# Gate stage: the residual rows are added by accumulating transfers, and each tile is finished one pair later

## The chip, the cores and the metric

The kernel runs on one core of one Trainium2 chip. The metric is the device time of one execution in microseconds. A core has a matrix engine (PE, with its weight loads shown as PEld), a vector engine (DVE), a scalar engine (ACT), a general engine (POOL) and a sync engine (SP) that only issues transfers. Each executes its own instructions in order; semaphores tie them together. Transfers are issued from the queues of SP, POOL and ACT and are carried out by 16 DMA engines that all queues share.

## The reference

One layer of a streaming encoder over 2048 prompt rows and 32 sample rows of width 1024:

```
hn = rmsnorm(h);  proj = hn @ w_in
yA, yB = short-conv mixer(proj), pooling mixer(proj)
h = h + concat[yA, yB] @ w_out
gate = sigmoid(rmsnorm(h) @ w_ple_gate)
h = h + (p @ w_ple) * gate
y = rmsnorm(h) * g_final
```

All of it is in 32-bit floating point, and the small state outputs of the two mixers are returned too. The change touches only the last two lines: `h + e*gate` with `e = p @ w_ple`, and the final norm.

## The kernel before

The rows are cut into 16 tiles of 128 rows (0 to 15) and one of 32 rows (16). Products are made at full precision from pairs of rounded numbers: each operand is split into a high and a low part, and three matmuls stand for one. Pairs of tiles are multiplied with seven block products instead of eight, after Strassen and Winograd, in the function `seven`.

The program has three stages. The first makes the input projection and the mixers, about 0 to 520 us. The second multiplies by w_out and adds the input, giving h, which is stored in device memory as `h_d`; interleaved with it, e is made and stored as `e_d`. The third, the gate stage, starts at 729.6 us and works through the tiles in pairs: the pairs 0, 2, 4 to 12 in the loop at L1809, and the pair 14 with tile 15 in `last_pair`, which ends the program. The 32-row tile is done by itself between pairs 4 and 6 (`short_gate`).

For a pair i the gate stage does this. Two "frames" (`hn` tiles) are loaded from `h_d` ahead of time in `prep_g`: the upper tile i by one transfer (L396), the lower one i + 1 by four that rearrange it (L1512). The upper frame is copied by ACT (L1552) and transposed on PE (L1554, `pth`); the lower one is transposed on DVE (L1560). Sums and differences of the blocks are formed (L1743) and split into high and low parts (L81 on ACT, L84 on DVE). Then `seven` issues the products, 12 matmuls each, in the order 11, 12, S2, S1, S3, S4, 22; the places between them are numbered, and `following[st]` runs what is wanted at place st. Results in PSUM (X, Y, Z) are copied out by ACT (`c_g`, L1573) or added by DVE (L1581), and go through the sigmoid on ACT (L1582 or L1579). In `gate_ops`, DVE multiplies the half tile of e by the gate (L1584) and adds the product to the half tile of h (L1585), four times each for a pair. `done_g` then finishes a tile: ACT squares and sums it (L94), POOL makes the reciprocal root (L73 and L77), DVE multiplies by both factors (L1592), and the tile is stored to the output (L1593).

Tiles of 128 x 1024 live in rings: `xh` with four tiles holds the two h tiles of a pair, and `ya` with five holds frames and e tiles. A tile's place is free again when its last reader is done, which for a stored tile is when the store has landed. The order of instructions on each engine comes from a scheduler that works ahead of time with its own estimates of durations; `tc.keep_in_program_order` pins an instruction to its place in the program. Order is thus fixed at build time, and a wait at run time holds everything behind it on the same engine.

h tiles of pairs 0 to 4 are loaded from POOL's queue, the others from SP's. Output tiles 0 to 5 and 16 are stored from POOL's queue, 6 to 15 from SP's, the very last piece from ACT's.

Of the kernel before, what the change touches and what calls it, by code (L numbers as in the profile page):

```python
# [15 lines left out]
P = 128  # L16
# [20 lines left out]
def trunk(ctx, tc, x_p, x_s, c_conv, c_pool, p_p, p_s, g_mix, w_in, conv_w, conv_b, pool_w,  # L37
# [1266 lines left out]
    with ExitStack() as s2:  # L1304
# [202 lines left out]
        def by_quarters(i):  # L1507

            r, n = tiles[i]
            t = ring4(ya, f"hn_{i}")  # L1510
            for q in range(4):
                nc.sync.dma_start(t[q * 32:q * 32 + 32].rearrange("p (g c) -> p g c", g=4),  # L1512
                                  h_d[r:r + P, q * 256:q * 256 + 256].rearrange("(g p) c -> p g c", p=32))
            return t
# [53 lines left out]
        def gate_ops(h, e, n, name, i):  # L1568
            scale = lambda at: rs_h[:n, i + at[0]:i + at[0] + 1]

            def carry(ps, at):
                t = st.tile([P, NH], F32, tag="t", name=f"c_{name}_{at[0]}{at[1]}")
                carried.append(nc.scalar.copy(t[:n], ps[:n]))  # L1573
                return t

            def out(ps, c, at):
                if c is None:
                    c = st.tile([P, NH], F32, tag="t", name=f"g_{name}_{at[0]}{at[1]}")
                    nc.scalar.activation(c[:n], ps[:n], AF.Sigmoid, scale=scale(at))  # L1579
                else:  # L1580
                    nc.vector.tensor_tensor(c[:n], ps[:n], c[:n], op=ALU.add)  # L1581
                    nc.scalar.activation(c[:n], c[:n], AF.Sigmoid, scale=scale(at))  # L1582
                ee, hh = half_of(e, at, n), half_of(h, at, n)
                nc.vector.tensor_tensor(ee, ee, c[:n], op=ALU.mult)  # L1584
                nc.vector.tensor_tensor(hh, hh, ee, op=ALU.add)  # L1585

            return carry, out

        def done_g(i, h, later=False):
            r, n = tiles[i]  # L1590
            rf = sumsq(h, n, f"f{i}", later=later)
            nc.vector.scalar_tensor_tensor(h[:n], h[:n], rf[:n], g_bc[:n], op0=ALU.mult, op1=ALU.mult)  # L1592
            (nc.sync if 6 <= i < NT - 1 else nc.gpsimd).dma_start(rows_of(y_p, y_s, r, n), h[:n])  # L1593

        def short_ops(h, e, n):

# [13 lines left out]

            return carry, out

        def last_pair(i, A, before):

# [112 lines left out]
                weigh(1, cols_of(0))  # L1727
                normed(1, root(1))

            seven(f"g{i}", A, W, held, out, {1: chunk, 3: before, 4: rest, 5: upper_half}, first_tile=True, end=end)  # L1730

        def prep_g(i, ahead=False):

            A, got = {}, {}
            whole = lambda t: t.rearrange("p k (g t) -> p k g t", g=4)

            def put(q, src, view=lambda t: t):
                A[q] = cmb.tile([P, KH, 2, P], F32R, tag="c", name=f"g{i}_{q}")
                split(view(A[q][:, :, 0]), view(A[q][:, :, 1]), src)

            def comb(q, x, y, op, view=lambda t: t):
                t = ss.tile([P, KH, P], F32, tag="s", name=f"g{i}_f{q}")
                nc.vector.tensor_tensor(view(t), x, y, op=op)  # L1743
                return t

            lower = []

            def load():
                got["lower"] = by_quarters(i + 1) if i else first_lower
                got["upper"] = load_rows(ya, "hn", i, h_d) if i else first_h  # L1750

            if ahead:
                load()

            def first():
                if not ahead:
                    load()
                lower.extend(turned_here(got["lower"], not i))

            def second():  # L1760
                a21, a22 = lower
                s1 = comb("S1", a21, a22, ALU.add, whole)
# [12 lines left out]
            S[i] = A  # L1775
            return {2: first, 4 if i in (2, 8) else 3: second}
# [20 lines left out]
        def short_gate():  # L1797
# [7 lines left out]
            done_g(NT - 1, h)  # L1805
            yield

        short_steps = short_gate()
        for i in range(0, NT - 3, 2):  # L1809
            A = S.pop(i)  # L1810
            following = prep_g(i + 2, not i)
            h = [load_rows(xh, "h", i + b, h_d, queue=nc.gpsimd if i < 6 else nc.sync) for b in range(2)]
            e = [load_rows(ya, "e", i + b, e_d) for b in range(2)]
            seven(f"g{i}", A, W, *gate_ops(h, e, P, f"g{i}", i), following)
            done_g(i, h[0])
            if i in (0, 2, 4):
                next(short_steps)
            if i + 2 < NT - 3:
                done_g(i + 1, h[1])
        last_pair(NT - 3, S[NT - 3], lambda: done_g(NT - 4, h[1], True))  # L1820

# [1 line left out]
_INS = ['x_prompt', 'x_sample', 'cache_conv', 'cache_pool', 'p_prompt', 'p_sample', 'g_mix', 'w_in',  # L1823
# [25 lines left out]
```

## Time and profile before

| what | value |
|---|---|
| median of 3 runs | 909.32 us (908.84 to 909.93) |
| profiled execution, its own time | 909.97 us |
| profiled execution, span of instructions | 908.2 us |
| PE busy | 893.2 us, 98% of the span |
| DVE busy | 702.4 us, 77% |
| ACT busy | 460.1 us, 51% |
| POOL busy | 152.0 us, 17% |
| granted PE clock, mean | 0.998 |
| bytes moved | 198.5 MB, 219 GB/s over the span |

The span is that of the instructions; the execution's own time lies 1.8 us above it. A busy PE counts matmuls whose ends are modelled, so a share of 100% says that PE never ran out of work, not that it was at its peak. The rows of a tile or line give minimum, median and maximum duration in ns and the first and last start; the chain is the sequence of work that ended last, merged into pieces.

### The profile page before, as it was taken

What the parts mean: (1) busy time and instruction counts of PE and PEld (TensorE: products, weight loads), DVE (VectorE), ACT (ScalarE), POOL (GpSimd) and SP (SyncE); (2) the same over time, 40 slices, a digit from 0 to 9 for tenths busy, and PEclk for the clock granted to TensorE, in tenths of its full rate; (3) what the DMA queues carried; (4) which work ended last, traced back from release to release, by engine and by line L of the source; (5) the groups of instructions that cost most, each with busy time, mean ns of one, the idle gap of its engine ahead of it and who ended that gap; (6) DMA issues with size and microseconds to landing.
All of it is one profiled execution on the core that took longest, in us unless ns stands there. A gap on an engine that the chain in (4) does not pass through costs nothing.

```text
span 908.2 us, 12176 instructions
## 1 busy us (share of the span) xinstructions
PE 893.2 (98%) x4174; PEld 722.8 (80%) x4174; DVE 702.4 (77%) x1158; ACT 460.1 (51%) x834; POOL 152.0 (17%) x290
## 2 busy tenths in 40 slices
PE   8999999999999999999999999999999999999996
PEld 6788888888888887877778886888887888778885
DVE  6899799897993688846667579965565988897885
ACT  7744554554453345533444376544434865565554
POOL 2210122222121123100000020221111211120012
PEclk9999999999999999999999999999999999999999
DMA  8255286857699666667745496787677965565554
GB/s 268 63 188 172 84 262 204 246 157 226 179 340 424 176 222 200 215 222 225 264 136 175 163 331 198 255 259 250 199 274 254 342 244 176 184 228 196 185 193 168
DMA packets 113387, 198.52 MB, mean 219 GB/s; under 512 B 13174, under 2 KB 70062, under 8 KB 112429
## 3 DMA queue, kind: packets, MB, share of 16 engines
q1 hardware_dynamic: 91309, 124.72, 42.5%
q0 software_dynamic: 19568, 68.62, 22.2%
q10 hardware_dynamic: 2448, 4.39, 1.3%
q8 instruction: 33, 0.54, 0.3%
q14 instruction: 29, 0.24, 0.1%
HBM read 132.53 MB, written 65.15 MB: 218 GB/s over the span
## 4 chain that ended last, share of the span: by engine, by line
PE 73%; issue 11%; DMA 8%; DVE 3%; ACT 2%; POOL 2%; POOLq 0%; DVEq 0%; ACTq 0%
PE x_g L185 9%; PE x_o L185 8%; PE x_zab L646 6%; PE x_zbv L646 6%; PE x_ch L646 6%; PE z_g L185 5%; PE z_o L185 4%; DMA raw_zab_0b<-in_w_in_dram 4%; PE z_zab L646 3%; PE z_ch L646 3%; PE z_zbv L646 3%; PE e L109 2%; PE y_g L185 2%; PE y_o L185 2%; DMA B<-p_d 2%
## 5 line engine op out<-in xcount | busy, mean ns | idle before, releaser
L185 PE MATMUL z_o<-wo,y_S 128*128 128x512 f32 x192 | 47.4, 389 | 0.0
L185 PE MATMUL x_o<-wo_T,y_S 128*128 128x512 f32 x192 | 46.4, 391 | 0.6 <-DVE c_o L1319 0.6
L646 PE MATMUL x_zab<-B,w_zab_S 128*128 128x512 f32 x192 | 46.8, 392 | 0.2 <-DVE w_zab_S L84 0.2
L185 PE MATMUL z_g<-wg,g_S 128*128 128x512 f32 x192 | 46.8, 391 | 0.0
L646 PE MATMUL z_zab<-B,w_zab_S 128*128 128x512 f32 x192 | 46.8, 391 | 0.0
L185 PE MATMUL x_o<-wo,y 128*128 128x512 f32 x192 | 45.2, 390 | 0.0
L646 PEld LDWEIGHTS x_zab<-B,w_zab_S 128*128 128x128 f32 x192 | 35.8, 188 | 8.8 <-DVE w_zab_S L84 0.6
L185 PEld LDWEIGHTS x_o<-wo_T,y_S 128*128 128x128 f32 x192 | 35.9, 188 | 8.7 <-DVE c_o L1319 1.3
L185 PEld LDWEIGHTS x_o<-wo,y 128*128 128x128 f32 x192 | 36.1, 188 | 7.7
L646 PEld LDWEIGHTS z_zab<-B,w_zab_S 128*128 128x128 f32 x192 | 35.8, 188 | 7.8 <-DVE w_zab_S L84 0.3
L185 PEld LDWEIGHTS z_o<-wo,y_S 128*128 128x128 f32 x192 | 36.0, 188 | 7.5
L646 PE MATMUL x_ch<-B,w_ch_S 128*128 128x512 f32 x168 | 41.9, 393 | 0.0
L185 PEld LDWEIGHTS z_g<-wg,g_S 128*128 128x128 f32 x192 | 35.8, 188 | 7.5 <-ACT c_g L1573 0.2
L646 PE MATMUL x_zbv<-B,w_zbv_S 128*128 128x512 f32 x168 | 40.9, 393 | 0.3 <-ACT zs L986 0.3
L646 PE MATMUL z_zbv<-B,w_zbv_S 128*128 128x512 f32 x168 | 40.5, 390 | 0.0
L646 PE MATMUL z_ch<-B,w_ch_S 128*128 128x512 f32 x168 | 40.4, 390 | 0.0
L646 PEld LDWEIGHTS x_zbv<-B,w_zbv_S 128*128 128x128 f32 x168 | 31.3, 188 | 8.0 <-ACT zs L986 0.7
L646 PEld LDWEIGHTS x_ch<-B,w_ch_S 128*128 128x128 f32 x168 | 31.3, 188 | 7.3 <-ACT U L986 0.4
L646 PEld LDWEIGHTS z_ch<-B,w_ch_S 128*128 128x128 f32 x168 | 31.6, 188 | 6.6
L646 PEld LDWEIGHTS z_zbv<-B,w_zbv_S 128*128 128x128 f32 x168 | 31.5, 188 | 6.5
L81 ACT CAST y_S<-y_fS 128x512 fp32r<-128x512 f32 x28 | 17.0, 620 | 28.1 <-PE x_o L185 12.2
L1319 DVE TENSOR_TENSOR c_o<-x_o,x 128x512 f32<-128x512 f32 x14 | 9.6, 689 | 21.8 <-PE x_o L185 21.8
(552 smaller groups left out, 2288.9 us busy)
## 6 DMA issues: line engine op xcount, KB each, us to landing
wn<-in_w_in_dram SPq DMA_DIRECT2D x24, 512.0 KB, 4.8
y<-y_d SPq DMA_DIRECT2D x16, 512.0 KB, 6.8
p_dT<-T POOLq DMA_DIRECT2D x15, 512.0 KB, 5.1
e<-e_d SPq DMA_DIRECT2D x15, 512.0 KB, 4.1
x<-in_x_prompt_dram SPq DMA_DIRECT2D x14, 512.0 KB, 5.6
B<-p_d POOLq DMA_DIRECT2D x3, 2048.0 KB, 15.6
B<-p_dT POOLq DMA_DIRECT2D x3, 2048.0 KB, 21.5
h_d<-x SPq DMA_DIRECT2D x12, 512.0 KB, 7.1
```

The lines of the kernel that those rows point to most:

```text
L81: ins = nc.scalar.copy(hi, src)
L109: nc.tensor.matmul(ps, pps[:, a, k], wp[k][b][:, cs], start=k + q == 0, stop=k == 1 and q == 2)
L185: nc.tensor.matmul(ps[:n], lhs[:, k, a, :n], w[b][:, k], start=start and k + q == 0, stop=k == KH - 1 and q == 2, skip_group_check=True)
L646: nc.tensor.matmul(ps, lhs[:, k, x], b[:, k, y], start=start and k + q == 0, stop=stop and k == KH - 1 and q == 2, skip_group_check=True)
L1319: add = lambda o, a, b: nc.vector.tensor_tensor(o, a, b, op=ALU.add)
```

## The change

In the pairs of the loop, no h tile is loaded and DVE adds nothing onto it. Instead e is multiplied in place by the gate, and when both halves of a tile have been multiplied POOL's queue issues a transfer that reads the tile's rows of `h_d` and adds them onto e in on-chip memory (L1590 of the new file). That is one such transfer per tile, 14 of 512 KB in all. The finishing work `done_g` of a pair is no longer issued right after the pair but at places 4 and 6 of the next one, pinned to its place on ACT and now on DVE too; the last pair gets the finishing of tile 12 at its place 3 and of tile 13 at place 4. The pairs' e tiles sit in `ya` (except those of the first pair), frames from tile 4 on in `xh`. Outputs 0 to 11 are stored from POOL's queue, 12 to 15 from SP's. The 32-row tile and the last pair keep their loaded h and the add on DVE.

```diff
         def by_quarters(i):
             r, n = tiles[i]
-            t = ring4(ya, f"hn_{i}")
+            t = ring4(xh if i > 3 else ya, f"hn_{i}")
...
-                ee, hh = half_of(e, at, n), half_of(h, at, n)
+                ee = half_of(e, at, n)
                 nc.vector.tensor_tensor(ee, ee, c[:n], op=ALU.mult)
-                nc.vector.tensor_tensor(hh, hh, ee, op=ALU.add)
+                if h is not None:
+                    hh = half_of(h, at, n)
+                    nc.vector.tensor_tensor(hh, hh, ee, op=ALU.add)
+                elif at[0] + at[1] == 1:
+                    r = tiles[i + at[0]][0]
+                    nc.gpsimd.dma_start(e[at[0]], h_d[r:r + P], accum_op=ALU.add)
...
         def done_g(i, h, later=False):
             r, n = tiles[i]
             rf = sumsq(h, n, f"f{i}", later=later)
-            nc.vector.scalar_tensor_tensor(h[:n], h[:n], rf[:n], g_bc[:n], op0=ALU.mult, op1=ALU.mult)
-            (nc.sync if 6 <= i < NT - 1 else nc.gpsimd).dma_start(rows_of(y_p, y_s, r, n), h[:n])
+            ins = nc.vector.scalar_tensor_tensor(h[:n], h[:n], rf[:n], g_bc[:n], op0=ALU.mult, op1=ALU.mult)
+            if later:
+                tc.keep_in_program_order(ins)
+            (nc.sync if NT - 5 <= i < NT - 1 else nc.gpsimd).dma_start(rows_of(y_p, y_s, r, n), h[:n])
...
-            seven(f"g{i}", A, W, held, out, {1: chunk, 3: before, 4: rest, 5: upper_half}, first_tile=True, end=end)
+            seven(f"g{i}", A, W, held, out, {1: chunk, 3: sooner, 4: lambda: (before(), rest()), 5: upper_half}, first_tile=True, end=end)
...
-                got["upper"] = load_rows(ya, "hn", i, h_d) if i else first_h
+                got["upper"] = load_rows(xh if i > 3 else ya, "hn", i, h_d) if i else first_h
...
+        def joined(a, b):
+            def both(p, q):
+                def run():
+                    p()
+                    q()
+                return run
+            return {**a, **{st: both(a[st], f) if st in a else f for st, f in b.items()}}
+
         for i in range(0, NT - 3, 2):
             A = S.pop(i)
             following = prep_g(i + 2, not i)
-            h = [load_rows(xh, "h", i + b, h_d, queue=nc.gpsimd if i < 6 else nc.sync) for b in range(2)]
-            e = [load_rows(ya, "e", i + b, e_d) for b in range(2)]
-            seven(f"g{i}", A, W, *gate_ops(h, e, P, f"g{i}", i), following)
-            done_g(i, h[0])
+            e = [load_rows(ya if i else xh, "e", i + b, e_d) for b in range(2)]
+            if i:
+                following = joined(following, finish)
+            seven(f"g{i}", A, W, *gate_ops(None, e, P, f"g{i}", i), following)
+            finish = {st: lambda b=b, i=i, e=e: done_g(i + b, e[b], True) for b, st in enumerate((4, 6))}
...
-            if i + 2 < NT - 3:
-                done_g(i + 1, h[1])
-        last_pair(NT - 3, S[NT - 3], lambda: done_g(NT - 4, h[1], True))
+        last_pair(NT - 3, S[NT - 3], finish[4], finish[6])
```

The order of the instructions changes only from about the start of the gate stage on. Three places are shown: pair 4 on PE and SP, the first pairs on POOL, and the last pair on DVE and ACT. Names go by the tiles' numbers (`e_0` is the e tile of tile 0, `hn_6` the frame of tile 6, `g4` the products of pair 4, `f0` the final norm of tile 0).

The first is PE in pair 4, where the upper frame of tile 6 is transposed (`pth_6`). Before:

```order
L185 MATMUL x_g4_6937<-wq_6245,g4_S2_6811 128x512 x12
L185 MATMUL z_g4_6939<-wg_11_6219,g4_S1_6816 128x512 x12
L185 MATMUL x_g4_6937<-wg_T3_6494,g4_S3_6819 128x512 x12
L185 MATMUL z_g4_6939<-wg_21_6507,g4_S4_6822 128x512 x2
L1554 MATMUL pth_6_0_6994<-ident_75,ho_6_0_6995 128x128 x4
L1554 MATMUL pth_6_1_7001<-ident_75,ho_6_1_7002 128x128 x4
L185 MATMUL z_g4_6939<-wg_21_6507,g4_S4_6822 128x512 x10
L185 MATMUL x_g4_6937<-wq_6245,g4_22_6825 128x512 x12
```

Now:

```order
L185 MATMUL y_g4_6906<-wg_21_6507,g4_12_6781 128x512 x12
L185 MATMUL x_g4_6905<-wq_6245,g4_S2_6784 128x512 x12
L185 MATMUL z_g4_6907<-wg_11_6219,g4_S1_6789 128x512 x3
L1554 MATMUL pth_6_0_6961<-ident_75,ho_6_0_6962 128x128 x4
L185 MATMUL z_g4_6907<-wg_11_6219,g4_S1_6789 128x512 x2
L1554 MATMUL pth_6_1_6968<-ident_75,ho_6_1_6969 128x128 x4
L185 MATMUL z_g4_6907<-wg_11_6219,g4_S1_6789 128x512 x7
L185 MATMUL x_g4_6905<-wg_T3_6494,g4_S3_6792 128x512 x12
L185 MATMUL z_g4_6907<-wg_21_6507,g4_S4_6795 128x512 x12
L185 MATMUL x_g4_6905<-wq_6245,g4_22_6798 128x512 x12
```

The two groups of transposes stood inside the product S4 of pair 4; they now stand inside S1, some 5 us of products earlier.

The same place on SP's queue, where the frames are loaded. Before:

```order
L396 DMA e_4_6933<-e_d_59 128x1024
L396 DMA e_5_6935<-e_d_59 128x1024
L1512 DMA hn_7_6970<-h_d_58 32x4x256 x4
L396 DMA hn_6_6975<-h_d_58 128x1024
L396 DMA e_6_7174<-e_d_59 128x1024
L396 DMA h_6_7170<-h_d_58 128x1024
L396 DMA e_7_7176<-e_d_59 128x1024
L1512 DMA hn_9_7211<-h_d_58 32x4x256 x4
```

Now:

```order
L396 DMA e_4_6901<-e_d_59 128x1024
L396 DMA e_5_6903<-e_d_59 128x1024
L1512 DMA hn_7_6937<-h_d_58 32x4x256 x4
L396 DMA hn_6_6942<-h_d_58 128x1024
L1512 DMA hn_9_7172<-h_d_58 32x4x256 x4
L396 DMA hn_8_7177<-h_d_58 128x1024
L1512 DMA hn_11_7350<-h_d_58 32x4x256 x3
L396 DMA e_6_7136<-e_d_59 128x1024
```

The frames of tiles 8 and 9 now follow those of 6 and 7 directly, without e and h loads between. `hn_6` is now put in the place of `e_0`, and waits until the store of output tile 0 has landed; before, it waited only for DVE to have used `e_3` for the last time.

And POOL's queue from the first pair on. Before:

```order
L396 DMA h_1_6545<-h_d_58 128x1024
L396 DMA h_2_6722<-h_d_58 128x1024
L396 DMA h_3_6724<-h_d_58 128x1024
L73 TENSOR_SCALAR ms_f0_6706<-ssq_f0_6704 128x1
L77 TENSOR_TENSOR rstd_f0_6708<-ms_f0_6706,nhalf_83 128x1
L1593 DMA out_0_dram<-h_0_6543 128x1024
L73 TENSOR_SCALAR ms_f1_6716<-ssq_f1_6714 128x1
L77 TENSOR_TENSOR rstd_f1_6718<-ms_f1_6716,nhalf_83 128x1
L1593 DMA out_0_dram<-h_1_6545 128x1024
```

Now:

```order
L1590 DMA e_0_6543<-h_d_58 128x1024
L1590 DMA e_1_6545<-h_d_58 128x1024
L73 TENSOR_SCALAR ms_f0_6817<-ssq_f0_6815 128x1
L77 TENSOR_TENSOR rstd_f0_6819<-ms_f0_6817,nhalf_83 128x1
L73 TENSOR_SCALAR ms_f1_6856<-ssq_f1_6854 128x1
L1600 DMA out_0_dram<-e_0_6543 128x1024
L1590 DMA e_2_6700<-h_d_58 128x1024
L77 TENSOR_TENSOR rstd_f1_6858<-ms_f1_6856,nhalf_83 128x1
L1590 DMA e_3_6702<-h_d_58 128x1024
L1600 DMA out_0_dram<-e_1_6545 128x1024
```

The loads of h are gone, the accumulating transfers (L1590) stand in their place, later in the program, and the store of output tile 0 now stands behind the first step of tile 1's norm (`ms_f1`), which waits for the square of tile 1 on ACT.

The last place is DVE and ACT in the last pair. DVE before:

```order
L1585 TENSOR_TENSOR h_13_7724<-h_13_7724,e_13_7728 128x512
L1592 SCALAR_TENSOR_TENSOR h_12_7722<-h_12_7722,rstd_f12_7894,g_bc_89 128x1024
L1670 TENSOR_TENSOR c_g14_00_7923<-y_g14_7909,c_g14_00_7923 128x512
L1592 SCALAR_TENSOR_TENSOR h_13_7724<-h_13_7724,rstd_f13_7967,g_bc_89 128x1024
L1633 TENSOR_TENSOR c_g14_00_7923<-e_14_7900,c_g14_00_7923 128x512
L1634 TENSOR_TENSOR h_14_7902<-h_14_7902,c_g14_00_7923 128x512
L1670 TENSOR_TENSOR c_g14_01_7961<-z_g14_7910,c_g14_01_7961 128x512
L1633 TENSOR_TENSOR c_g14_01_7961<-e_14_7900,c_g14_01_7961 128x512
L1670 TENSOR_TENSOR c_g14_11_7983<-x_g14_7908,c_g14_11_7983 128x512
```

DVE now:

```order
L1597 SCALAR_TENSOR_TENSOR e_11_7494<-e_11_7494,rstd_f11_7828,g_bc_89 128x1024
L1677 TENSOR_TENSOR c_g14_00_7873<-y_g14_7859,c_g14_00_7873 128x512
L1640 TENSOR_TENSOR c_g14_00_7873<-e_14_7850,c_g14_00_7873 128x512
L1641 TENSOR_TENSOR h_14_7852<-h_14_7852,c_g14_00_7873 128x512
L1597 SCALAR_TENSOR_TENSOR e_12_7670<-e_12_7670,rstd_f12_7917,g_bc_89 128x1024
L1597 SCALAR_TENSOR_TENSOR e_13_7672<-e_13_7672,rstd_f13_7939,g_bc_89 128x1024
L1677 TENSOR_TENSOR c_g14_01_7911<-z_g14_7860,c_g14_01_7911 128x512
L1640 TENSOR_TENSOR c_g14_01_7911<-e_14_7850,c_g14_01_7911 128x512
L1677 TENSOR_TENSOR c_g14_11_7933<-x_g14_7858,c_g14_11_7933 128x512
```

ACT before:

```order
L94 ACTIVATE junk_90,ssq_f12_7890<-h_12_7722 128x1024
L1573 COPY c_g14_01_7961<-x_g14_7908 128x512
L94 ACTIVATE junk_90,ssq_f13_7963<-h_13_7724 128x1024
L1666 ACTIVATE c_g14_00_7923<-c_g14_00_7923,rs_h_88 128x512
L1573 COPY c_g14_11_7983<-z_g14_7910 128x512
L1638 ACTIVATE junk_90,ssq_l0_0_7985<-h_14_7902 128x512
L1666 ACTIVATE c_g14_01_7961<-c_g14_01_7961,rs_h_88 128x512
```

ACT now:

```order
L1573 COPY c_g14_01_7911<-x_g14_7858 128x512
L94 ACTIVATE junk_90,ssq_f12_7913<-e_12_7670 128x1024
L1573 COPY c_g14_11_7933<-z_g14_7860 128x512
L94 ACTIVATE junk_90,ssq_f13_7935<-e_13_7672 128x1024
L1645 ACTIVATE junk_90,ssq_l0_0_7943<-h_14_7852 128x512
L1673 ACTIVATE c_g14_01_7911<-c_g14_01_7911,rs_h_88 128x512
```

The final multiplications of tiles 12 and 13 (L1592, now L1597) both stand ahead of the sum `c_g14_01` on DVE, as they did before, but the squares on which they rest come one product later on ACT and read tiles that the accumulating transfers of pair 12 have just completed.

More of the change, by code (lines that the diff above doesn't have):

```diff
@@ L1611, in short_ops, with last_pair @@
             return carry, out
-        def last_pair(i, A, before):
+        def last_pair(i, A, sooner, before):
             pps = load_pps(ss.tile([P, 2, 2, P], F32R, tag="s", name="pps_l"), i + 1, nc.sync)
```

## The prediction

> **What bounds the kernel.** I read part 1 of the page first, then the busy times by stretch of the gate stage, then the waits of PE in it, then the chain.
>
> ```profile
> PE 893.2 (98%) x4174; PEld 722.8 (80%) x4174; DVE 702.4 (77%) x1158; ACT 460.1 (51%) x834; POOL 152.0 (17%) x290
> ```
>
> ```profile
> core 0: us, PE busy (x) PEld busy (x) DVE busy (x) ACT busy (x) POOL busy (x), PEclk, DMA share, GB/s
> 729.60:750.00 20.40, 20.40 (x96) 16.92 (x95) 16.40 (x27) 13.15 (x23) 2.40 (x5) 1.00 0.65 231
> 750.00:770.00 20.00, 20.00 (x97) 16.20 (x96) 15.67 (x23) 11.90 (x23) 3.24 (x7) 1.00 0.62 196
> 770.00:790.00 20.00, 20.00 (x94) 16.62 (x93) 15.79 (x25) 9.86 (x19) 3.90 (x7) 1.00 0.63 210
> ...
> 880.00:900.50 20.50, 20.47 (x107) 17.28 (x105) 16.82 (x26) 11.91 (x26) 4.56 (x9) 1.00 0.52 184
> 900.50:908.20 7.70, 0.00 (x0) 0.00 (x0) 2.09 (x4) 1.29 (x5) 0.95 (x3) 0.73 0.24 91
> sum 178.60, PE 170.87 PEld 138.98 DVE 142.38 ACT 97.90 POOL 26.23; mean PE 17.09 PEld 13.90 DVE 14.24 ACT 9.79 POOL 2.62
> ```
>
> From 729.6 to 900.5 us PE is busy 170.87 of 170.9 us at full granted clock (1.00), and the waits view names no wait of PE in that stretch. DVE is busy 140.3 us (142.38 less 2.09), or 82%. The matmuls are the same before and after. So work taken from DVE is worth nothing by itself; the stage can only lose, by making PE wait, and every wait of PE is paid in full, since no later idle time takes it up. Behind the last matmul stand 7.7 us of finish and stores.
>
> **The part that is removed.** Rows of the h tiles:
>
> ```profile
> L1585 DVE TENSOR_TENSOR h<-h,e x30: 651/684/695, 738.5 to 885.3; 128x512 f32<-128x512 f32 x28, 32x512 f32<-32x512 f32 x2
> L94 ACT ACTIVATE junk<-h x15: 1042/1058/1070, 751.5 to 887.0; 128x1024 bf16<-128x1024 f32 x14, 32x1024 bf16<-32x1024 f32 x1
> L94 ACT ACTIVATION_READ_ACCUMULATOR junk<-h x15: 185/187/201, 752.4 to 888.0; 128x1 f32 x14, 32x1 f32 x1
> L1592 DVE SCALAR_TENSOR_TENSOR h<-h,rstd_f,g_bc x15: 1232/1285/1286, 753.6 to 889.1; 128x1024 f32<-128x1024 f32 x14, 32x1024 f32<-32x1024 f32 x1
> ...
> L396 POOL DMA_DIRECT2D h<-h_d x6: 527/532/577, 729.3 to 781.0; - x6
> ```
>
> 28 full adds of 0.684 us go from DVE: 19.2 us. They lie beside PE throughout, so 0 on the path. The 14 loads of h (8 on SP, 6 on POOL) go too, and 14 transfers that add come on POOL: the same bytes from memory, the same number of issues.
>
> ```profile
> q0 software_dynamic: 19568, 68.62, 22.2%
> ...
> h<-h_d SPq DMA_DIRECT2D x10, 512.0 KB, 5.8
> ...
> hn<-h_d SPq DMA_DIRECT2D x8, 512.0 KB, 4.5
> ...
> h<-h_d POOLq DMA_DIRECT2D x6, 512.0 KB, 5.2
> out_dram<-h POOLq DMA_DIRECT2D x6, 512.0 KB, 3.6
> ```
>
> POOL's queue moved 68.62 MB in 22.2% of 908.2 us of all 16 engines, which is 340 GB/s: a 512 KB transfer costs the engines 1.54 us. The trace has no accumulating transfer. Its bounds: no more engine time than a plain one (0 added), or that of two more, a read and a write of the tile (14 x 3.1 = 43 us over 171, which takes the DMA share from about 0.6, the last column but one above, to 0.85). I take one more, 1.54 us each, since the tile must be read as well as written: 22 us, a share of about 0.7, which leaves room on average. What counts is where one must have landed, or holds up another.
>
> The Trainium skill, in "DMA: Bandwidth & Descriptors", Rules for kernel authors, says that an accumulating transfer reads its destination and writes it later. That fits the middle value; no run here shows it. By the figures of the Trainium skill's same page (section on the anatomy of one DMA: 2.0 us and bytes over 436 GB/s), an estimate for twice 512 KB is 4.4 us, and then the terms of both places below would be 0; the trace's plain transfers already take longer than that.
>
> **The finish one pair later.** The same squares, roots, multiplications and stores, moved. In the loop an accumulating transfer is issued when a tile's second half has been multiplied, and its square stands 11 to 16 us later (behind 4 and 6 products of 2.72 us of the next pair). The slowest plain transfer from `h_d` took 9.5 us (below), so here the wait costs nothing; and what a late square would hold up on ACT, the splits for the next pair, PE reads a further 10 us later. Two places have less room.
>
> **Pair 4.** The frame of tile 6 takes the place of `e_0` and waits for output tile 0 to be stored. PE's times in the chain of before hold for the new order at the ends of products S4 of pair 2 and S2 of pair 4, since only transposes move between:
>
> ```profile
> 764.11 2.72 PE z_g L185 x12
> ...
> 776.17 2.72 PE x_g L185 x12
> 778.89 2.72 PE z_g L185 x12
> ...
> 784.78 0.88 PE pth L1554 x8
> ...
> 886.43 2.72 PE z_g L185 x12
> ```
>
> ```profile
> 768.81 0.68 DVE L1581 TENSOR_TENSOR c_g<-z_g,c_g 128x512 f32<-128x512 f32 x1
> ...
> 773.12 1.75 SPq L1512 DMA_DIRECT2D hn<-h_d  x4
> ...
> 775.27 0.34 SPq L396 DMA_DIRECT2D hn<-h_d  x1
> 775.33 0.19 POOL L73 TENSOR_SCALAR ms_f<-ssq_f 128x1 f32<-128x1 f32 x1 [12.71 <-ACT junk L94]
> ...
> 778.31 0.72 ACT L1582 ACTIVATE c_g<-c_g,rs_h 128x512 f32<-128x512 f32 x1 [1.75 <-DVE c_g L1581]
> ...
> 782.13 1.14 ACT L1552 COPY ho<-hn 128x512 f32<-128x512 f32 x2
> ```
>
> Before, the frame was asked for at 775.3 and PE wanted it at 784.8. Now: S4 of pair 2 ends at 766.8; the DVE sum (0.68) and the sigmoid (0.72) end at 768.3 with the hand-overs; the square of tile 1, which stands ahead of tile 0's store by way of POOL's order, ends 1.06 + 0.19 later, 769.6; `ms_f1` 0.19: the store goes out at 769.85 (tile 0's own multiplication, 1.29 from 768.2, is done by then). PE reaches the transposes after three matmuls of S1, at 778.9 + 0.7 = 779.6, and the copy on ACT takes 0.57, so store and load together may take 9.05 us. The medians give 3.6 + 4.5 = 8.1. With the accumulating transfers of tiles 2 and 3 issued at about 770.4 and 771.5 beside them, I add the engine time of one, 1.54: 9.65, a wait of 0.6 us. The ends, by the rows of all transfers to the output and from `h_d` (minimum, median, maximum):
>
> ```profile
> DMA to landing us min/median/max: 2.3/3.5/8.5
> ...
> DMA to landing us min/median/max: 2.5/4.5/9.5
> ```
>
> 2.3 + 2.5 gives no wait; 8.5 + 9.5 gives 9 us. Of the later frames only those of tiles 9 and 13 wait for a store. Tile 1's goes out at about 772.9, one multiplication after tile 0's and two gate steps on, so tile 9's frame is asked for near 777; its transpose on DVE feeds products that start past 810. The e tiles wait for stores too, but of two pairs earlier, and are asked for at least 7 us before DVE wants them by the same count. Nothing is charged for these. Behind the waiting `hn_6` on SP stand just these frames and e tiles. On POOL the transfer that adds onto tile 2 waits for DVE ahead of tile 1's root; that puts off tile 1's finish by a few tenths, which no product waits for.
>
> **The last pair.** DVE's sum onto X must be done before PE adds the last product onto the same bank:
>
> ```profile
> 886.52 0.59 ACT L1573 COPY c_g<-x_g 128x512 f32<-128x512 f32 x1 [1.33 <-PE x_g L185]
> ...
> 889.24 0.57 ACT L1573 COPY c_g<-z_g 128x512 f32<-128x512 f32 x1
> ...
> 892.90 0.69 DVE L1670 TENSOR_TENSOR c_g<-z_g,c_g 128x512 f32<-128x512 f32 x1 [1.19 <-PE z_g L185]
> ...
> 894.52 1.52 PE L109 MATMUL e_l<-wl,pps_l 128*128 128x512 f32 x6
> 894.99 0.69 DVE L1670 TENSOR_TENSOR c_g<-x_g,c_g 128x512 f32<-128x512 f32 x1
> ```
>
> The sum ended at 895.7, PE's `e_l` at 896.04: 0.3 us of room. Now ACT copies at 889.24 to 889.8 and squares tile 13 until 891.1; POOL's 0.19 + 0.56 end at 892.0, DVE's 1.29 at 893.3, and the sums start 0.4 later than before (893.3 for 892.9). 0.4 less 0.3: PE waits 0.1 us. This needs tile 13's accumulating transfer by 889.8. It goes out after pair 12's last gate, 878.3 (the start of S1 of pair 14, 886.4 in the chain, less three products) + 0.7 for the sigmoid + 0.7 for the multiplication + about 0.5 for its turn on POOL: 880.2. So it has 9.6 us; the median plain one of POOL's is 5.2, with its own second read 6.7. In time.
>
> Issues on POOL: each transfer takes about 0.53 us there (the row above), against 12 us of idle time between roots (12.71 in the row at 775.33): nothing. The output stores of tiles 6 to 11 go from SP to POOL, which frees SP for the last weights; `e_l` did not wait for them before: nothing.
>
> **The sum.** 909.97 (profiled execution) + 0.6 + 0.1 = 910.7; by the runs' median, 0.65 lower: 910.0 us. 0.2% of the time is 1.8 us, about what a measurement of this kernel can tell from no change.
>
> **Rivals.** First, the frame of tile 6 comes so late that PE waits more than 1.8 us in pair 4: it decides from 10.9 us for store and load. For it: stores up to 8.5 and loads up to 9.5 us are in the trace. Against: the medians. With 6 + 6.5 us, 3.5 us: 912.8.
>
> Second, accumulating transfers are slow, and the last pair waits for tile 13's: it decides past 9.6 us, and each us more goes to PE whole, by the square, the root and the pinned multiplication ahead of the sums. For it: a plain load from `h_d` took up to 9.5, and two stores and the weights of the last product share these microseconds. With 11 us it is 1.4, and the same slowness adds 1.5 more in pair 4: 912.9; at twice the slowest plain one, 19 us, 9.4: 919.
>
> Third, faster: the shorter DVE work brings PE something or shortens the tail. Against: PE's idle time to 900.5 is 0.03 us and no instruction of the 7.7 us behind it goes. It would take a quarter of that tail: 907.3.
>
> Fourth, the change does nothing that shows, all waits covered: 909.3, within the forecast.
>
> **Chances.** The forecast, fourth rival included, 0.56, its own range 908.7 to 911.1; first rival 0.18, second 0.21, third 0.05. So faster 0.05, same 0.56, slower 0.39. The range reaches from 908.6 to 914.5: above it lie the long ends of both slow rivals, about 0.1, below it the third.
>
> **What will show it.** Right: 14 rows L1590 on POOL, none on DVE for the adds; PE's waits in the gate stage hold `pth` in pair 4 with about 0.6 us and nothing over 1 us; `hn_6` asked for near 773.4. Wrong: a wait of PE for DVE before the last products (second rival), landings of L1590 over 9.6 us, or a `pth` wait in another pair, which would mean that the stores feed the frames later than worked out.

## The result, and the profile after

The changed kernel took 920.88 us (median of 4 runs, 918.55 to 921.81), the kernel before 909.08 us (4 runs, 908.37 to 909.93): a ratio of 1.0122, 95% interval 1.0105 to 1.0139. It is slower by 1.2%, where 910.0 us had been forecast, and it lies above the range (908.6 to 914.5). The profiled execution took 921.81 us, its span 920.0 us.

Part 1 of the page after, then the waits of PE in the gate stage:

```profile
PE 897.5 (98%) x4174; PEld 725.9 (79%) x4174; DVE 686.3 (75%) x1130; ACT 460.8 (50%) x834; POOL 164.3 (18%) x304
```

```profile
engine line waited for: us in total, times, longest us
PE pth L1554 <- ACT ho L1552: 4.4, 1, 4.4
PE x_g L1722 <- DVE c_g L1677: 1.6, 1, 1.6
PE x_g L185 <- DVE c_g L1581: 0.7, 1, 0.7
PE x_g L185 <- ACT c_g L1573: 0.7, 1, 0.7
```

DVE has 28 instructions less, as forecast, and 16 us less (702.4 before), where the forecast had added up 19.2; PE, which waited nowhere in this stage, now waits in four places. The busy times by stretch show where (the columns as in the prediction: busy time of each engine, granted clock, share of the DMA engines, GB/s):

```profile
core 0: us, PE busy (x) PEld busy (x) DVE busy (x) ACT busy (x) POOL busy (x), PEclk, DMA share, GB/s
750.00:770.00 20.00, 20.00 (x94) 16.64 (x93) 14.39 (x23) 12.10 (x22) 2.54 (x4) 1.00 0.47 112
770.00:790.00 20.00, 15.56 (x72) 12.50 (x72) 9.49 (x14) 6.91 (x13) 4.14 (x6) 0.92 0.69 172
...
810.00:830.00 20.00, 18.58 (x85) 14.93 (x84) 12.40 (x19) 10.57 (x20) 2.07 (x5) 1.00 0.65 196
830.00:890.00 60.00, 60.00 (x278) 49.96 (x278) 45.70 (x66) 34.77 (x61) 15.70 (x26) 1.00 0.70 197
890.00:913.20 23.20, 21.55 (x111) 17.90 (x109) 12.79 (x18) 10.06 (x21) 8.33 (x14) 1.00 0.77 242
```

The three losses: 4.4 us in pair 4 (770 to 790), 1.4 us in pair 6 (810 to 830), 1.6 us in the last pair (890 to 913.2). In the first of these stretches the granted clock is 0.92: PE idles, and from 786.8 to 790.2 us the clock is 0.50; the matmuls right behind the pause start 0.43 to 0.57 us apart in place of 0.23.

For the comparisons below I cut each span in three, by the starts of matmuls in the trace: up to the first matmul of the gate (`x_g`), from there to the last matmul, and from there to the end.

| profile | up to the gate | gate | end | span |
|---|---|---|---|---|
| before | 729.5 | 170.7 | 8.0 | 908.2 |
| after | 733.1 | 179.8 | 7.2 | 920.0 |

Of the 11.8 us, 9.0 lie in the gate. Cut at the first matmul into `y_g` of each pair, pair 2 is 0.3 us shorter than before, pair 4 is 6.0 longer (the pause, then three 128x512 matmuls and eight transposes at half rate), pair 6 is 1.8 longer, and the pairs behind it 1.6 together. The end gives 0.8 back. The 3.6 us ahead of the gate belong to no instruction that the change touches; the first experiment is on them.

The rows behind the wait in pair 4, from the timelines of POOL, SP, ACT and PE (start, duration, engine, line, tiles, and what ended the idle time before):

```profile
start us, us, engine line op out<-in xcount [idle before <-releaser]
773.72 0.62 POOL L1600 DMA_DIRECT2D out_dram<-e  x1
774.34 0.91 POOL L1590 DMA_DIRECT2D e<-h_d  x1
...
775.45 1.23 POOL L1590 DMA_DIRECT2D e<-h_d  x1
777.46 0.57 POOL L1600 DMA_DIRECT2D out_dram<-e  x1 [0.78 <-DVE e L1597]
...
777.32 0.34 SPq L396 DMA_DIRECT2D hn<-h_d  x1
...
786.60 0.62 ACT L1552 COPY ho<-hn 128x512 f32<-128x512 f32 x1 [5.60 <-DMA hn<-h_d]
...
787.27 1.12 PE L1554 MATMUL pth<-ident,ho 128*128 128x128 f32 x4 [4.43 <-ACT ho L1552]
```

Tile 0's store goes out at 773.72 and lands 3.55 us later; the frame of tile 6 is asked for at 777.32, at once. But ACT gets it at 786.60, 9.28 us later, and PE waits. Between 774 and 778 the two transfers that add onto tiles 2 and 3 and the store of tile 1 go out beside it; the second adding transfer lands at 786.24, 0.36 us before ACT's copy.

### The profile page after: what moved, and what is told of

Same layout as the page of the kernel before. It is cut to its first block, busy times and chain, and to the rows that moved or that the text cites. A ratio compares the mean times of both kernels' runs of the same rounds, so it can differ in the third digit from the quotient of the medians.

```text
span 920.0 us, 12147 instructions
## 1 busy us (share of the span) xinstructions
PE 897.5 (98%) x4174; PEld 725.9 (79%) x4174; DVE 686.3 (75%) x1130; ACT 460.8 (50%) x834; POOL 164.3 (18%) x304
## 3 DMA queue, kind: packets, MB, share of 16 engines
q0 software_dynamic: 21584, 75.96, 26.4%
## 5 line engine op out<-in xcount | busy, mean ns | idle before, releaser
L1597 DVE SCALAR_TENSOR_TENSOR e<-e,rstd_f,g_bc 128x1024 f32<-128x1024 f32 x14 | 18.0, 1283 | 12.8 <-POOL rstd_f L77 9.7
```

Of the source, the lines that this page charges most:

```text
L1597: ins = nc.vector.scalar_tensor_tensor(h[:n], h[:n], rf[:n], g_bc[:n], op0=ALU.mult, op1=ALU.mult)
```

## The experiments

**Again.** The changed kernel unaltered, for a second profile.

> The changed kernel once more, with nothing altered. Its first profile was 11.8 us longer than that of before, and 3.7 us of it stand ahead of the gate stage, where both programs issue the same instructions in the same order. Theory one, that these 3.7 us have nothing to do with the change: in a second profile PE reaches the gate stage with another offset, anything from 0 to 4 us, and the waits of PE in the gate stage come back as they were: pth in pair 4 at 4.0 to 4.8 us, two waits of about 0.7 us in pair 6, 1.5 us ahead of the last products; 918 to 922 us. Theory two, that the change moves something ahead of the gate after all: again 3.5 to 4 us of offset, with the same eight matmuls at 0.43 us near 555 us.

919.57 us (5 runs), ratio 1.0098 [1.0082, 1.0114]. The gate began at 728.7 us, 0.8 earlier than before where the first profile had it 3.6 later; the waits in the gate came back (4.6, 0.8, 0.7, 1.9 us). So theory one holds: the offset ahead of the gate is chance. Gate and end together are 8.2 us longer than before in the first profile and 10.1 in this one, where the medians differ by 11.8 and 9.5. In the first profile PE stood idle for 1.3 us near 553 us (two matmuls 1.84 us apart) and the eight matmuls behind that started 0.43 us apart, where the profile before shows 1.0 us idle at the same place (1.37 us apart) and none of these. This second profile has nine such matmuls behind the wait in pair 4, the first had three; pair 4 is 1.5 us longer again, most of it by these, in a gate of 181.7 us. The Trainium skill, "TensorE: Matmul & The Clock Gate", Part 1, says that the clock is halved after an idle window of about 3.4 us and that the windows run free, so that the same kernel meets a different number of slow matmuls each time; the halved rate and the changing number agree (a granted clock of 0.50 for 3.4 us in the first profile, for 6.8 in this one), while the 1.3 us of idle time near 553 us are shorter than such a window.

**Plain transfers in place of adding ones.**

```
-                    nc.gpsimd.dma_start(e[at[0]], h_d[r:r + P], accum_op=ALU.add)
+                    nc.gpsimd.dma_start(e[at[0]], h_d[r:r + P])
```

> The 14 adding transfers become plain ones from h_d over the same tiles (the sum of h and e*gate is left out: the tile then holds h alone); order, tiles, queues and waits stay. Theory A, the adding transfers are slow and slow down what runs beside them (first of a pair 5.4 to 8.1 us, second 9.2 to 10.8 us, hn_6 beside two of them about 9 us): the L1590 rows fall to 3 to 6 us, the load of hn_6 to 4 to 6 us, PE's wait for pth in pair 4 to under 1 us, the waits of pair 6 and the last pair to under 0.5 us together; 909 to 912 us. Theory B, the order is to blame (frames behind stores, finishes a pair later) whatever the transfers cost: the same waits, 917 us or more.

914.73 us (5 runs), 1.0048 [1.0035, 1.0061]: neither theory alone. The waits of PE, then the L1590 transfers and POOL's queue, of this kernel:

```profile
engine line waited for: us in total, times, longest us
PE pth L1554 <- ACT ho L1552: 2.6, 1, 2.6
```

```profile
L1590 POOL DMA_DIRECT2D e<-h_d x14: 527/535/583, 751.1 to 883.6; - x14
...
DMA to landing us min/median/max: 4.5/6.2/8.4
...
q0 software_dynamic: 21584, 75.96, 24.8%
```

and the same of the changed kernel:

```profile
L1590 POOL DMA_DIRECT2D e<-h_d x14: 850/928/1284, 754.1 to 891.4; - x14
...
DMA to landing us min/median/max: 5.4/7.3/10.8
...
q0 software_dynamic: 21584, 75.96, 26.4%
```

The waits of pair 6 and of the last pair are gone, so these need the adding. The one in pair 4 falls from 4.4 us to 2.6 and is not gone: `hn_6` took 7.2 us from issue to copy (774.64 to 781.86) even beside plain transfers. (Of the 4.3 us of this profile over that of before, 2.6 lie in the gate and 1.2 at the end, where the last store goes out 3.5 us behind the start of the last matmul, as before, and the execution ends 5.7 us after it in place of 4.5.) The price of adding comes out too: 26.4% of 920.0 us less 24.8% of 912.5 us is 16.6 us of all 16 engines, or 1.2 us for each of 14 transfers, and it takes POOL 0.93 us to issue one in place of 0.53. The same shows where `hn_6` is under way (columns as above, the last two being the share of the DMA engines and GB/s). The changed kernel:

```profile
775.00:785.00 10.00, 7.83 (x35) 6.14 (x33) 4.30 (x5) 1.31 (x2) 2.25 (x4) 1.00 1.01 230
```

and this one:

```profile
775.00:785.00 10.00, 7.38 (x37) 5.72 (x36) 4.02 (x6) 3.42 (x6) 0.00 (x0) 1.00 0.77 238
```

About as many bytes a second move (230 and 238 GB/s), but with the adding transfers the 16 engines are busy throughout (a share of 1.01), with plain ones at 0.77.

**The first pair in the old way.**

```
+            h = [load_rows(xh, "h", b, h_d, queue=nc.gpsimd) for b in range(2)] if not i else None
-            e = [load_rows(ya if i else xh, "e", i + b, e_d) for b in range(2)]
-            if i:
+            e = [load_rows(ya, "e", i + b, e_d) for b in range(2)]
+            if i > 2:
                 following = joined(following, finish)
-            seven(f"g{i}", A, W, *gate_ops(None, e, P, f"g{i}", i), following)
+            seven(f"g{i}", A, W, *gate_ops(h, e, P, f"g{i}", i), following)
+            if not i:
+                for b in range(2):
+                    done_g(b, h[b])
```

> The first pair alone goes back to the old way: h loaded into the ring of four, e into the ring of five, the sum on DVE, both tiles finished in their own pair; twelve adding transfers stay. Theory A with the frame behind the store: the place of hn_6 is then free a pair earlier, its load is asked for long before 777 us, PE's wait for pth in pair 4 (4.4 us, with about 1 us of slow matmuls behind it) is gone, the waits of pair 6 and the last pair (1.4 and 1.6 us) stay: 914 to 917 us. Rival: the adding transfers of tiles 2 and 3 alone make hn_6 late, whenever it is asked for: pth still waits 3 us or more, 918 to 921 us.

911.16 us (12 runs), 1.0011 [1.0001, 1.0021]: better than expected.

```profile
engine line waited for: us in total, times, longest us
PE x_g L1722 <- DVE c_g L1677: 1.9, 1, 1.9
```

`hn_6` is asked for at 762.77 and copied at 769.45; nobody waits for it. The waits of pair 6, which I had expected to stay, are gone as well: the four quarters of tile 11's frame now go out together at 780.26, ahead of the e tiles (the next run shows what they stood behind). This edit changes both when the first pair's stores land and which places the frames and e tiles take, so it does not tell the two apart. With the run before, the order (a frame behind a store, with its load in the middle of other transfers) sets off the waits, and the adding makes them dearer.

**The transposes on DVE in program order.**

```
-                lower.extend(turned_here(got["lower"], not i))
+                lower.extend(turned_here(got["lower"], True))
```

> The transposes of the lower frames on DVE are held in program order, so that the one of tile 11 stands in pair 8 and no longer in pair 6, where DVE waited 5.1 us for it. Theory C, pair 6 waits because that transpose stands ahead of the sums on DVE, and its frame's last quarter stands on SP behind e_6, which waits for the store of tile 2: the two waits of PE in pair 6 (0.7 us each, with what the matmuls behind them lose 2.1 us) go, all others stay; 918 to 920 us, 1.4 to 2.1 us under the run of the changed kernel beside it. Rival: pair 6 is late because of the squares of tiles 4 and 5 behind their adding transfers: the two waits stay, no gain.

917.91 us (6 runs), 1.0082 [1.0065, 1.0099], and the profile shows both waits of pair 6 gone:

```profile
engine line waited for: us in total, times, longest us
PE pth L1554 <- ACT ho L1552: 3.4, 1, 3.4
PE x_g L1722 <- DVE c_g L1677: 1.6, 1, 1.6
```

Theory C stands. In the changed kernel the chain reads like this (timelines of SP, DVE and PE):

```profile
805.26 0.34 SPq L396 DMA_DIRECT2D e<-e_d  x1
805.65 1.80 SPq L1512 DMA_DIRECT2D hn<-h_d  x1
...
815.55 1.25 DVE L1560 STREAM_TRANSPOSE hn<-hn 128x1024 f32<-128x1024 f32 x1 [5.08 <-DMA hn<-h_d]
...
819.80 3.03 PE L185 MATMUL x_g<-wg_T,g_S 128*128 128x512 f32 x12 [0.70 <-ACT c_g L1573]
...
826.95 3.04 PE L185 MATMUL x_g<-wq,g 128*128 128x512 f32 x12 [0.72 <-DVE c_g L1581]
```

`e_6` stands on SP ahead of the last quarter of tile 11's frame and waits until the store of tile 2 has landed (805.2). The quarter goes out at 805.65 beside two adding transfers; DVE, which transposes this frame a whole pair before it is needed, stands still until 815.55 with the sums of pair 6 behind it.

**Tile 13 finished behind the sums** (the kernel with the first pair in the old way, and in `last_pair`):

```
-            seven(f"g{i}", A, W, held, out, {1: chunk, 3: sooner, 4: lambda: (before(), rest()), 5: upper_half}, first_tile=True, end=end)
+            seven(f"g{i}", A, W, held, out, {1: chunk, 3: sooner, 4: rest, 5: lambda: (upper_half(), before())}, first_tile=True, end=end)
```

> As the kernel with the first pair in the old way (911.2 us, one wait left: 1.9 us ahead of the last products), and tile 13's finish moved behind the two sums onto X: its square, root and multiplication no longer stand ahead of them. Theory, tile 13's adding transfer is what these sums waited for (by the square, the root and the pinned multiplication): the wait falls under 0.3 us, PE's last matmul comes about 2 us earlier; tile 13's store lands later, which may lengthen the tail behind the last matmul from 7.2 to 8 or 9 us: 909 to 911 us. Rival, the sums are late for another reason (the weights of the last product, the stores): the wait stays at 1.5 to 2 us, 911 us or more.

909.85 us (12 runs), 0.9997 [0.9985, 1.0009]. No wait of PE in the gate is listed any more, the gate takes 170.5 us, the end 8.7. Tile 13's transfer, by its square, root and multiplication, was what the sums waited for. In the profiles this moves the time to the end rather than saving it: gate and end together take 179.2 us, as with the first pair in the old way alone (172.0 and 7.2), although the medians are 1.3 us apart. In the changed kernel (timelines of ACT, DVE and PE):

```profile
902.35 1.06 ACT L94 ACTIVATE junk<-e 128x1024 bf16<-128x1024 f32 x1 [1.74 <-DMA e<-h_d]
...
904.44 1.29 DVE L1597 SCALAR_TENSOR_TENSOR e<-e,rstd_f,g_bc 128x1024 f32<-128x1024 f32 x1 [2.53 <-POOL rstd_f L77]
905.65 0.68 DVE L1677 TENSOR_TENSOR c_g<-z_g,c_g 128x512 f32<-128x512 f32 x1
...
907.73 0.68 DVE L1677 TENSOR_TENSOR c_g<-x_g,c_g 128x512 f32<-128x512 f32 x1
...
908.47 1.69 PE L1722 MATMUL x_g<-wq,g 128*128 128x256 f32 x12 [1.58 <-DVE c_g L1677]
```

**Each adding transfer in two halves.**

```
-                elif at[0] + at[1] == 1:
+                else:
                     r = tiles[i + at[0]][0]
-                    nc.gpsimd.dma_start(e[at[0]], h_d[r:r + P], accum_op=ALU.add)
+                    nc.gpsimd.dma_start(ee, h_d[r:r + P, at[1] * NH:at[1] * NH + NH], accum_op=ALU.add)
```

> The changed kernel with each adding transfer cut in two of 256 KB, each issued as soon as its half of the tile has been multiplied, so that the first halves go out some 8 us earlier. Theory A, what counts is how much is left to be added when a pair ends: the last transfer of a tile lands 5 to 7 us after its issue (9 to 11 before), the wait ahead of the last products (1.6 to 1.9 us) goes, pth's in pair 4 (4.5 us) falls to 2 to 3: 913 to 917 us. Rival, the fixed part of each transfer and the 14 further issues of 0.9 us on POOL eat this up: landings of 8 us and more for half the bytes, waits as before, 918 to 922 us.

911.73 us (12 runs), 1.0009 [0.9996, 1.0022], better than theory A asked. One wait is left, in pair 4:

```profile
engine line waited for: us in total, times, longest us
PE pth L1554 <- ACT ho L1552: 1.5, 1, 1.5
```

The same bytes are added, but half of them 5 to 13 us earlier (756.4 and 765.5 for tiles 2 and 3, where whole tiles went out at 769.9 and 771.0 in the second profile of the changed kernel), and what a frame or a square meets is the smaller remainder: `hn_6` takes 5.6 us (773.22 to 778.80). That each landing still takes a median 5.7 us for half the bytes (7.3 for whole tiles) does not matter.

**Stores on SP.**

```
-            (nc.sync if NT - 5 <= i < NT - 1 else nc.gpsimd).dma_start(rows_of(y_p, y_s, r, n), h[:n])
+            (nc.sync if i < NT - 1 else nc.gpsimd).dma_start(rows_of(y_p, y_s, r, n), h[:n])
```

> The changed kernel with all its output stores but the short one's on SP in place of POOL. Theory of the queue: the store of tile 1 took 10.2 us (3.6 for tile 0's) because it stood behind two adding transfers on POOL's queue; on SP it lands in 4 to 6 us, the frames of tiles 9 and 8 are asked for 4 us earlier, the waits of pair 6 (0.7 and 0.8 us) shrink or go. Theory of the engines: while two adding transfers run, all 16 engines are busy (share 1.0), whatever the queue: still 8 to 10 us, same waits. In both hn_6 is as late as before (pth 3.5 to 5 us): 916 to 921 us.

916.49 us (6 runs), 1.0061 [1.0042, 1.0080]. The store of tile 1 goes out at 772.3 and the frame of tile 9, which waits for it on SP, at 777.70: at most 5.4 us, for 10.2 on POOL's queue. The waits of pair 6 are gone, as the theory of the queue had it. But the two stores are not alike: in the changed kernel it stood behind both adding transfers on POOL's queue, here it goes out 0.9 us ahead of the second (773.19). One store of this run goes out on SP behind both and has its landing on record:

```profile
846.83 1.79 POOL L1590 DMA_DIRECT2D e<-h_d  x2 [8.90 <-DVE e L1584]
...
850.87 0.34 SPq L1600 DMA_DIRECT2D out_dram<-e  x1
...
DMA to landing us min/median/max: 8.1/8.1/8.1
```

It lands 1.2 us after the second of them. In the profile after, the five stores behind both on POOL's queue took 6.8 to 11.3 us and landed 1.2 to 2.5 us after the second. So what this run changes is the place ahead of the second adding transfer; that the queue itself matters is not shown. The Trainium skill, "DMA: Bandwidth & Descriptors", section on queues, rings and completion order, says that each engine serves its queue rows in turn, a packet at a time; these landings do not show it. `hn_6` still needs 8.7 us on SP's own queue, and `pth` waits 2.4 us, with the last pair at 2.2 and one wait of 0.5 us in a later pair.

**Both remedies**, the first pair in the old way and the halves:

> The first pair in the old way and the twelve adding transfers cut in two. If pair 4's frame and tile 13's transfer are the two causes that are left, PE then waits nowhere in the gate stage: 909 to 910.5 us, no measurable difference from before, since nothing that was removed was on the path. If slow adding transfers cost something that the waits of PE do not show: 911 us or more. Under 908.2 us would mean that the shorter DVE work is worth something after all.

908.10 us (12 runs), ratio 0.9971 [0.9961, 0.9982]: faster than before, by 0.3%. No wait of PE is left in the gate. Once more, on another chip:

> The version with the first pair in the old way and the adding transfers cut in two, once more (908.1 us, ratio 0.9971 [0.9961, 0.9982] the first time). Its first profile against that of before: from the first product of the gate to the last matmul 169.9 us for 170.7, from there to the end 7.2 for 8.0. Theory, a real gain of some 1.5 us: 908 to 909 us, ratio under 0.999, the same two differences. Rival, chance between executions: ratio across 1.000.

908.61 us (12 runs), 0.9985 [0.9973, 0.9996]. The stretches, with a second profile of the kernel before:

| profile | up to the gate | gate | end |
|---|---|---|---|
| before | 729.5 | 170.72 | 8.0 |
| before, second | 728.5 | 170.69 | 8.0 |
| both | 730.2 | 169.93 | 7.2 |
| both, second | 733.3 | 169.93 | 7.2 |

> The kernel of before once more, for a second profile. If its small gaps and its end belong to it: again 170.5 to 171 us from the first gate product to the last matmul and 7.8 to 8.1 us behind it. If they are chance: other values, as near as 0.3 us to 169.9 and 7.2.

909.0 us (one run). In these two kernels what varies between executions lies ahead of the gate. The two other stretches repeat to within 0.03 us, so 0.8 us less in the gate and 0.8 us less at the end are real. Of the gate's share 0.33 us lie in pair 2 (21.11 us before, 20.78 in both profiles of this version and of the changed kernel): there PE breaks off its products three times for transposes before and twice now, since the 32-row tile's are done in one group (at 770.16) in place of two (766.76 and 769.16). The rest is spread over the small hand-overs of 0.1 us at the ends of products. At the end the last store goes out at the same place, 3.5 us behind the start of the last matmul, and the execution ends 3.7 us after it in place of 4.5; why stays open.

**DVE's load put back** (both remedies, and one idle addition behind each half multiplication):

```
                 nc.vector.tensor_tensor(ee, ee, c[:n], op=ALU.mult)
+                if h is None:
+                    nc.vector.tensor_tensor(c[:n], c[:n], c[:n], op=ALU.add)
```

> That version with one more DVE instruction behind each of its 24 half multiplications, an addition of 128x512 over a tile that nobody reads any more: DVE carries the load of before again (about 0.68 us each), everything else stays. Theory D, the gain comes from DVE answering PE sooner at the ends of products: the stretch from the first gate product to the last matmul grows back from 169.9 to 170.5 us or more, 909 to 910 us. Rival, the gain is one of order and of the end alone: within 0.3 us of the run beside it.

910.04 us (12 runs), 0.9995 [0.9985, 1.0004], and a gate of 172.6 us, with waits where there were none:

```profile
engine line waited for: us in total, times, longest us
PE z_g L185 <- ACT c_g L1573: 0.9, 2, 0.7
PE x_g L1724 <- DVE c_g L1679: 0.7, 1, 0.7
```

The stretch grows by 2.6 us (172.57 less 169.93), more than theory D asked. All of it lies in the three pairs with a listed wait (0.66 in pair 2, 0.98 in pair 8, 1.00 in the last); the other pairs take as long as with the relief, to 0.02 us, and the end is again 7.2 us. So in this order DVE has no room for its old load, but the 0.8 us in the gate and the 0.8 us at the end are not shown to come from the relief. In the last pair the late piece is again tile 13's transfer, for which ACT's square waits 0.8 us: its second half goes out 0.6 us later against PE's products and takes 9.2 us in place of 8.2. (The medians differ by 1.4 us; what varies ahead of the gate is in both.)

**Only the later finish**, without adding transfers (h loaded and added on DVE as before; finishes from pair 2 on in the next pair):

```
+            if i > 2:
+                following = joined(following, finish)
...
-            done_g(i, h[0])
+            if not i:
+                for b in range(2):
+                    done_g(b, h[b])
+            finish = {st: lambda b=b, i=i, h=h: done_g(i + b, h[b], True) for b, st in enumerate((4, 6))}
...
-            if i + 2 < NT - 3:
-                done_g(i + 1, h[1])
...
```

> One part of the change alone: h is loaded and added on DVE as before, frames and e stay in the ring of five, and only the finish of a tile moves to the next pair (from pair 2 on). The h tiles then live a pair longer in the ring of four, and those of the last pair wait for stores of pair 12. Theory, finishing a pair later costs nothing where a tile is there in time: no wait of PE before the last pair; the last pair waits for its second h tile, 1 to 4 us: 910 to 914 us. Rival, later finishes get in the way of splits and sums on ACT and DVE in every pair: PE waits in several pairs, 914 us or more.

919.05 us (4 runs), 1.0097 [1.0077, 1.0117]. The rival has it. PE waits three times for transposes (2.9 us together) and once for a split:

```profile
engine line waited for: us in total, times, longest us
PE pth L1554 <- ACT ho L1552: 2.9, 3, 1.3
PE x_g L185 <- DVE g L84: 2.8, 1, 2.8
```

The split's place, in the timelines of DVE and PE:

```profile
880.36 1.28 DVE L1592 SCALAR_TENSOR_TENSOR h<-h,rstd_f,g_bc 128x1024 f32<-128x1024 f32 x1 [0.44 <-POOL rstd_f L77]
881.56 1.24 DVE L1560 STREAM_TRANSPOSE hn<-hn 128x1024 f32<-128x1024 f32 x1
...
884.49 0.68 DVE L84 TENSOR_TENSOR g<-pth,g 128x512 fp32r<-128x512 f32 x1
...
885.23 3.52 PE L185 MATMUL x_g<-wg,g 128*128 128x512 f32 x10 [2.82 <-DVE g L84]
```

DVE is busy from 880.4 on: the pinned multiplication of a tile of the pair before, a transpose and the additions of h stand ahead of the split that PE needs. Finishing later is thus not free where DVE still adds h; the version with both remedies finishes twelve tiles later, without those additions, and loses nothing. This fits the run with the idle additions: it is in the new order that DVE's 16 us are worth something. (The h tiles also live a pair longer in their ring here; this run does not price that by itself.)

## Why the prediction was wrong, step by step

The step that failed is the size of the waits for transfers: what a load, a store or an adding transfer takes when several are under way. The sum has 6.0 us for the load of `hn_6`, nothing for the other frames and e tiles, and 6.7 us for tile 13's adding transfer. Measured were 9.28 us, 1.8 us of lost time in pair 6, and 10.8 us.

*Bound.* PE carries the stage and pays every wait in full: right. It pays more than the wait, by the slow matmuls behind it (6.0 us in pair 4 for a pause of 4.4).

*Engine time of an adding transfer.* 1.54 us was taken, 1.2 us measured: the middle value was near. The Trainium skill, "DMA: Bandwidth & Descriptors", Rules for kernel authors, says that the destination is read and written later; the 1.2 us fit that, and no run here shows the read by itself. The conclusion, "leaves room on average", was the trap: the losses fall where several transfers meet, and there the share is 1.01.

*Pair 4.* The time at which `hn_6` would be asked for was right to a few tenths (773.4 plus the 3.6 us by which this execution was late is 777.0; 777.32 measured), and so was the store (3.6; 3.55). The term that failed is the load, 4.5 + 1.54 = 6.0 us in the sum, 9.28 in the trace: 3.2 us. The room was smaller as well, 8.45 us (from the store's issue, 773.72, to where PE stood still, 782.84, less 0.67 for the copy) in place of 9.05; that is the other 0.6 us between 0.6 and 4.4. (The terms that the 9.05 came from, 779.6 less 0.57 less 769.85, give 9.18.) I added the engine time of one transfer where two adding ones and a store stood beside it; with plain ones in their place it is 7.2 us, with halves 5.6. The first rival (from 1.8 us of wait) is what happened, at 4.4.

*"Nothing is charged for these."* This is the step that was wrong in kind. I counted when each e tile and frame would be wanted by a product, not where DVE's transpose of it stands, and missed that tile 11's last quarter is queued on SP behind `e_6`, which waits for a store. It cost 1.8 us, and holding the transposes in program order takes it away.

*Last pair.* The limit for tile 13's transfer, 9.6 us, was good: at 8.4 us and less (plain transfers) nothing waits, at 10.8 PE waits 1.6. The 6.7 us that I took for it was the mis-sized term. The second rival's mechanism, and nearly its price (1.4 us at 11 us), came true.

*The rivals and the range.* I gave the two slow rivals chances of their own, but adding transfers that crowd the others set off both, and a third place besides. Together they are 9.0 us in the gate, less 0.8 at the end, in the first profile; the range took in one at a time, and 3.6 us of that execution lie ahead of the gate by chance.

*Faster.* A small gain exists, and the losses hid it: 0.8 us in the gate and 0.8 at the end, seen once the waits were removed. It is not shown to be the third rival's mechanism, the lighter load of DVE: with that load put back the end keeps its 7.2 us and the pairs without a wait keep their time, and with plain transfers, where DVE has the same relief, the end takes 9.15.

## What to carry to other kernels

A transfer that takes work off an engine is not free because that engine's work was hidden: look for what its queue and the shared DMA engines then deliver later, at each place where a load waits for a store. Size a load by the transfers that are under way beside it, not by the median of the whole span plus one. And when buffers are re-used sooner, read the order of every engine for work that stands early in front of something urgent, since a late tile stalls all that is queued behind it.

## What the hardware showed beyond that

An adding transfer of 512 KB from POOL keeps POOL busy for 0.93 us (plain: 0.53) and costs 1.2 us more time of all 16 engines; of the two of a pair the first landed, in the profile after, 5.4 to 8.1 us after its issue, the second 9.2 to 10.8 in six pairs of seven (6.2 in the first). A store behind both landed 1.2 to 2.5 us after the second, on POOL's queue (five in the profile after) and on SP's (one with its landing on record). After a pause PE ran three 128x512 matmuls at half rate in one execution and nine in the next, with the same pause of 4.4 to 4.6 us; a pause of 2.4 us (stores on SP) was followed by eight, one of 2.6 us (plain transfers) by none. So one profile of such a wait does not give its price.
